# Operands formed a step ahead, another order of the seven products with eight PSUM banks, and output weights that stay split

## The chip, the cores and the metric

The kernel runs on one core of one Trainium2 chip. It has a matrix engine (TensorE, "PE" in the profile, its weight loads "PEld"), a vector engine (VectorE, "DVE"), a scalar engine (ScalarE, "ACT"), GpSimd ("POOL") and a sync engine ("SP") that here only starts DMAs. Each engine takes its instructions strictly in the order in which the kernel issued them. The metric is the device time of one execution in microseconds, the median over runs.

## The reference

One step of a decoder layer, for 1024 prompt tokens and 8 × 4 sample tokens that share the weights. The middle (convolution, state space and attention branches) is not touched by the change and is left out here.

```python
D_MODEL = 1024; D_FF = 2816
h = rmsnorm(x, g_pre_mix) * (1 + sc_m) + sh_m
merged = ...                                   # three branches of h @ w_in, each gated
x = x + g_m * rmsnorm(merged @ w_out, g_post_mix)
hf = rmsnorm(x, g_pre_ffn) * (1 + sc_f) + sh_f
gu = hf @ w_ffn_in                             # 1024 -> 2 * 2816
f = silu(gu[..., :D_FF]) * gu[..., D_FF:]
x = x + g_f * rmsnorm(f @ w_ffn_out, g_post_ffn)
```

## The kernel before

The 1056 tokens (1024 prompt, 32 sample) lie on the free axis in four chunks c of 264; features lie on the 128 partitions. Products are fp32 quality made of three matmuls of rounded operands: every weight tile and every activation tile is split into a high part (a ScalarE copy) and a low part (VectorE: the value less its high part), and PE adds high·high, high·low and low·high. So one 128 × 128 weight tile against one chunk is three matmuls of 128 × 264.

**The planner.** `run()` (L357-430) walks a list of atoms, each a group of matmuls into one PSUM bank. For each it issues the weight loads on SP, the split of weight units that come due (`split`, L382), the atom's matmuls, then the evacuation of the atom before (`pending`), and then lets side generators go on (`side.advance`): each yields a number of microseconds of atoms after which its next step is issued. The order of issue is the order on each engine. `dense` atoms have 24 matmuls, atoms of a job of the FFN's first matrix 12, atoms of its second matrix 33.

The change touches what is issued after 1122 us of the profile; there the stages are these.

- **Output projection** (L1957-1963): four chunks × eight tiles m of 128 output features, 24 matmuls each. Each of the 32 atoms loads, splits and uses its weight again (`split`: ScalarE `whi` L393, VectorE `wlo` L394), though the weights of c = 0 to 3 are the same. The evacuation `sq_gated` (L1805) squares the bank on ScalarE, writes the gated value `y` on ScalarE, and adds the square into `ss` on VectorE. When a chunk is through, `res_gen(c)` (L1825) makes the two RMS norms and the residual of that chunk: a small `s` matmul of `ss` with ones, a chain of 13 tiny VectorE instructions for the reciprocal root (L436-452), `rs_dg`, another `s` matmul, VectorE products and sums over `y` and `xc`, and the same again for the norm before the FFN. The four run one after another in a queue (`todo`, L1931). PSUM is shared as six banks z for atoms and two s for these small products.
- **FFN in, plain** (`plain_job`, L2003): four of the 22 column tiles as dense atoms, 16 atoms for token half p = 0 and then 16 for p = 1. `res_gen(2)` and `res_gen(3)` run beside the first 16.
- **FFN in, seven products** (`in_job`, L2030): 18 jobs. A job takes gate and up weights of one tile pair and forms 2 × 2 block products of halves with seven products q instead of eight (Strassen's way, in Winograd's form). Operand q is a half tile or a VectorE sum or difference of such (`make`, L2044; tile names `raw`, `ru`, `s`), which `halves` (L1982) splits into `wop`: ScalarE copies the high part, VectorE subtracts. Each operand serves two atoms (p = 0, 1) against the activations `ORDER[q]` (L1967). The evacuation (L2062) combines the products in `st`; at q = 6 follow Tanh, a product and a product (silu·up), and in every second job four subtractions and a store to DRAM `fd` from POOL.
- **FFN out, seven products** (L2146 on): products q = 0 to 5, each four tiles mi × two p atoms of 33 matmuls, then q = 6. Its weight operands come in three pieces per mi (`out_operand`, L2183), sums S kept in four tiles; its activations are read back from `fd` and split (`b_load` L2121, `b_split` L2133, lines L2135 and L310, names `mh`, `ml`, `xa`). `gated` (L2221) squares and gates a finished output, `last_gen(c)` (L2260) makes the last norm and residual, partly on POOL, and stores.

```python
RY = (4.5, 2.5, 4, 2)                                               # L46: the steps of res_gen
key = (p, {2: 0, 5: 3, 6: 4}.get(q, q))                             # L2092: products that share a bank
ORDER = ('B11', 'B21', 'T2', 'T3', 'T1', 'T4', 'B22')               # L1967
if q == 2: TT(g[:, h0], job['s'], g[:, h0], ALU.subtract)           # L2048, right before halves()
act.activation(out=w[:, 0:n], in_=src, func=AF.Copy, scale=scale)   # L1984, halves()
```

## Time and profile before

| | |
|---|---|
| median of 3 runs | 2056.93 us (2053.38 to 2059.02) |
| profiled execution | 2050.83 us, its span 2049.1 us |
| PE busy | 1910.2 us (93%), mean granted clock 0.966 |
| DVE busy | 1358.9 us (66%) |
| ACT busy | 730.8 us (36%) |
| POOL busy | 216.9 us (11%) |
| DMA | 288.50 MB, mean 141 GB/s |

PE is busy nearly throughout, and a busy PE is not one at full rate: its rows also last longer when it is fed late or when its clock is granted at the lower of its levels. The stretch that the change touches, 1122 us to the end, has to be read by stage.

### The profile page before, as it was taken

Reading aid. Unit: us, or ns where it says so; the run is one execution under the profiler, and the core shown is the slowest. Engines: PE = TensorE matmul, PEld = TensorE weight load, DVE = VectorE, ACT = ScalarE, POOL = GpSimd, SP = SyncE. Lnnn points to the kernel's source line nnn. Section 1 sums busy time; section 2 is a strip of 40 time slices with the busy share of each in tenths; the row PEclk is TensorE's granted clock in tenths of the full one; section 3 lists DMA queues with packets and bytes.
Section 4 is the critical chain, followed back from the end, with each engine's and each line's share of the span. In section 5 each row is a group of like instructions: output and inputs, shape, how many; then the busy total and the mean of one; then the engine's idle time right before and its main releaser. Section 6 shows DMA issues by size and latency. Waiting matters only on the chain. (4 is left out here: it accounts for less than half of the span.)

```text
span 2049.1 us, 33598 instructions
## 1 busy us (share of the span) xinstructions
PE 1910.2 (93%) x13440; PEld 1777.1 (87%) x13440; DVE 1358.9 (66%) x2795; ACT 730.8 (36%) x1418; POOL 216.9 (11%) x365
## 2 busy tenths in 40 slices
PE   8999999999998999998999888899999999999785
PEld 2899798798876899997999888899999999999785
DVE  5687684474474686565866677776666666666676
ACT  3422422422422542222233564433332333453442
POOL 0000001001010142213100000100000001101013
PEclk9999999999999999999999999999999999999897
DMA  7333133234354453327532555632232223666543
GB/s 288 81 104 107 45 135 136 80 107 144 119 199 179 174 165 122 109 90 219 150 106 82 176 196 194 214 124 99 79 115 95 79 84 123 233 200 235 164 159 120
DMA packets 90156, 288.50 MB, mean 141 GB/s; under 512 B 15876, under 2 KB 22116, under 8 KB 87312
## 3 DMA queue, kind: packets, MB, share of 16 engines
q1 hardware_dynamic: 53552, 144.79, 22.1%
q0 software_dynamic: 29104, 115.11, 16.2%
q10 hardware_dynamic: 7344, 26.47, 3.9%
q8 instruction: 105, 1.72, 0.3%
q14 instruction: 51, 0.42, 0.1%
HBM read 219.09 MB, written 68.15 MB: 140 GB/s over the span
## 5 line engine op out<-in xcount | busy, mean ns | idle before, releaser
L307 PE MATMUL z<-mh,wop 128*128 128x264 f32 x2024 | 401.1, 292 | 18.3 <-ACT mh L2135 9.6
L307 PE MATMUL z<-hh,whi 128*128 128x352 f32 x1152 | 379.7, 330 | 2.6 <-ACT hh L620 1.4
L307 PE MATMUL z<-hh,wlo 128*128 128x352 f32 x1152 | 372.5, 323 | 3.1 <-DVE wlo L394 3.1
L307 PE MATMUL z<-hl,whi 128*128 128x352 f32 x1152 | 372.2, 323 | 1.1 <-DVE hl L310 1.1
L307 PE MATMUL z<-ml,wop 128*128 128x264 f32 x1408 | 350.8, 291 | 3.2 <-DVE ml L310 3.2
L307 PEld LDWEIGHTS z<-mh,wop 128*128 128x128 f32 x2024 | 334.1, 196 | 20.9 <-ACT mh L2135 10.3
L394 DVE SCALAR_TENSOR_TENSOR wlo<-raw,whi 128x1024 fp32r<-128x1024 f32 x148 | 180.4, 1222 | 170.8 <-ACT whi L393 169.9
L307 PEld LDWEIGHTS z<-ml,wop 128*128 128x128 f32 x1408 | 250.9, 195 | 4.7 <-DVE ml L310 4.4
L307 PEld LDWEIGHTS z<-hh,whi 128*128 128x128 f32 x1152 | 218.7, 190 | 14.4 <-issue 6.9
L393 ACT ACTIVATE whi<-raw 128x1024 fp32r<-128x1024 f32 x148 | 156.1, 1056 | 189.1 <-PE z L307 158.6
L307 PEld LDWEIGHTS z<-hl,whi 128*128 128x128 f32 x1152 | 218.9, 190 | 3.1 <-DVE hl L310 2.0
L307 PEld LDWEIGHTS z<-hh,wlo 128*128 128x128 f32 x1152 | 218.1, 189 | 3.7 <-DVE wlo L394 3.7
L1503 DVE SCALAR_TENSOR_TENSOR ycv<-cub,vecs,ycv 128x1024 f32<-128x1024 f32 x120 | 153.9, 1282 | 3.1
L1984 ACT ACTIVATE wop<-raw 128x512 fp32r<-128x512 f32 x150 | 90.2, 614 | 177.8 <-DVE raw L310 98.9
L307 PE MATMUL z<-mh,whi 128*128 128x264 f32 x384 | 115.5, 301 | 4.6 <-ACT whi L393 4.6
L307 PE MATMUL z<-xa,wop 128*128 128x264 f32 x792 | 113.6, 293 | 4.0 <-ACT xa L2135 1.6
L307 PE MATMUL z<-mh,wlo 128*128 128x264 f32 x384 | 113.2, 295 | 2.2 <-DVE wlo L394 2.2
L307 PE MATMUL z<-ml,whi 128*128 128x264 f32 x384 | 112.5, 293 | 0.0
L307 PEld LDWEIGHTS z<-xa,wop 128*128 128x128 f32 x792 | 105.7, 196 | 5.3 <-ACT xa L2135 1.8
L310 DVE TENSOR_TENSOR wop<-raw,wop 128x512 fp32r<-128x512 f32 x90 | 61.9, 689 | 53.0 <-ACT wop L1984 52.8
L307 PEld LDWEIGHTS z<-mh,whi 128*128 128x128 f32 x384 | 76.3, 199 | 5.3 <-ACT whi L393 5.0
L307 PEld LDWEIGHTS z<-mh,wlo 128*128 128x128 f32 x384 | 75.9, 198 | 3.2 <-DVE wlo L394 3.1
(431 smaller groups left out, 3605.4 us busy)
## 6 DMA issues: line engine op xcount, KB each, us to landing
raw<-i_win SPq DMA_DIRECT2D x48, 512.0 KB, 3.7
raw<-i_wfi SPq DMA_DIRECT2D x43, 512.0 KB, 4.2
raw<-i_wfo SPq DMA_DIRECT2D x80, 256.0 KB, 3.1
fd<-ft POOLq DMA_DIRECT2D x22, 792.0 KB, 5.4
raw<-i_wmod SPq DMA_DIRECT2D x32, 512.0 KB, 4.3
raw<-i_wout SPq DMA_DIRECT2D x32, 512.0 KB, 3.8
gd<-g ACTq DMA_DIRECT2D x24, 528.0 KB, 2.9
g<-gd ACTq DMA_DIRECT2D x24, 528.0 KB, 4.8
```

Of the source, the lines that this page charges most:

```text
L307: return pe.matmul(out=out, lhsT=lhsT, rhs=rhs, start=start, stop=stop, **kw)
L310: dve.tensor_tensor(out=out, in0=a, in1=b, op=op)
L393: act.activation(out=hi[:, 0:n], in_=raw[:, 0:n], func=AF.Copy, scale=scale)
L394: dve.scalar_tensor_tensor(out=lo[:, 0:n], in0=raw[:, 0:n], scalar=scale, in1=hi[:, 0:n].bitcast(F32), op0=ALU.mult, op1=ALU.subtract)
L1503: dve.scalar_tensor_tensor(out=a_, in0=ub[:, k:k + TP], scalar=wv[:, k:k + 1], in1=a_, op0=ALU.mult, op1=ALU.add)
L1984: act.activation(out=w[:, 0:n], in_=src, func=AF.Copy, scale=scale)
```

## The change

Four edits. (1) `later` and `flush`: some instructions are no longer issued where they are written, but at the next operand's split or ahead of the next weight-using atom's matmuls: VectorE's low part of an operand or of an activation, the addition of squares, gating, Tanh and what follows it. A new function `pre` of an operand forms its sum or difference; it is issued when the operand *before* it is split. (2) `ORDER` is (B11, B21, T1, T2, T3, B22, T4), products that share a bank are now 0 and 3, 2 and 5, 4 and 6, Tanh follows q = 5, q = 2 is copied by ScalarE and q = 4 takes two VectorE additions; all eight PSUM banks are for atoms in this stage. (3) In the output projection the split weights of m = 4 to 7 stay in SBUF after c = 0 (`kept`); PSUM is shared four and four; the four `res_gen` run side by side, each started as its chunk ends, with other steps (`RY`); squares are added in pairs, and the last addition of `y` is left to PE, which takes two matmuls in place of one; `xc` lies in other tiles. (4) In the output stage S and the reloaded residual lie in twelve small tiles, `last_gen` is issued an atom later, and the loads and splits of the first activations are spread otherwise. In numbers, PE has 36 small matmuls more, DVE 48 instructions less, ACT 24 more, POOL 20 DMAs more and SP 12 weight loads less.

```diff
-RY = (4.5, 2.5, 4, 2)
+RY = (6, 3, 6, 2)
+    late_ops = []
+    def later(fn):
+        late_ops.append(fn)
+    def flush():
+        now = late_ops[:]
+        late_ops.clear()
+        for fn in now:
+            fn()
...
         def split(v):
             if op:
+                flush()
+                if v + 1 < len(units) and units[v + 1][3]:
+                    units[v + 1][3]['pre']()
                 parts[v] = wp.tile([128, 1024], F32R, tag=tags(v)[0], name="wop")
                 op['make'](parts[v])
                 return
             raw = raws.pop(v)
-            hi = wp.tile([128, 1024], F32R, tag="whi", name="whi")
-            lo = wp.tile([128, 1024], F32R, tag="wlo", name="wlo")
+            if keep:
+                hi, lo = keep()
+            else:
+                hi = wp.tile([128, 1024], F32R, tag="whi", name="whi")
+                lo = wp.tile([128, 1024], F32R, tag="wlo", name="wlo")
...
+            if a_.units:
+                flush()
             ps = a_.mm([parts[u] for u in a_.units])
...
-        open_psum(6, 2)
+        open_psum(4, 4)
...
         def rest():
-            if not first:
+            if i % 2 and i > 1:
                 TT(R_['ss', c], R_['ss', c], sq, ALU.add)
...
         TT(y[:, 0:4], y[:, 0:4], y[:, 4:8], ALU.add)
         TT(y[:, 0:2], y[:, 0:2], y[:, 2:4], ALU.add)
-        TT(y[:, 0], y[:, 0], y[:, 1], ALU.add)
         yield RY[2]
-        dg = rstd_bcast(rp, [y[:, 0, :]], 1024, EPS, 3)
+        dg = rstd_bcast(rp, halves_of(y), 1024, EPS, 3, place)
...
             if m == 7:
-                todo(res_gen(c), *([x_gen(0), x_gen(1)] if c == 3 else []))
+                R_['g', c] = side.add(res_gen(c))
+                if c == 3:
+                    R_['g', 4] = side.add(x_gens())
...
-            u = unit(flat(I['wout'][m]))
+            if c == 0 or m < 4:
+                u = unit(flat(I['wout'][m]), keep=kept(m) if m >= 4 else None)
+                if m >= 4:
+                    stay[m] = u
+            u = stay.get(m, u)
...
-    ORDER = ('B11', 'B21', 'T2', 'T3', 'T1', 'T4', 'B22')
+    ORDER = ('B11', 'B21', 'T1', 'T2', 'T3', 'B22', 'T4')
...
-            TT(w[:, 512:512 + n], src, w[:, 0:n].bitcast(F32), ALU.subtract)
+            later(lambda: TT(w[:, 512:512 + n], src, w[:, 0:n].bitcast(F32), ALU.subtract))
...
+        def pre(q):
+            def fn():
+                g, u = job['g'], job['u']
+                if q == 2:
+                    job['s'] = R_['fq'].tile([128, 512], F32, tag="s1", name="s1")
+                    TT(job['s'], u[:, h0], u[:, h1], ALU.add)
+                    TT(u[:, h0], g[:, h0], u[:, h0], ALU.subtract)
+                if q == 3:
+                    TT(g[:, h0], job['s'], g[:, h0], ALU.subtract)
+                if q == 5:
+                    TT(g[:, h1], g[:, h1], g[:, h0], ALU.subtract)
+            return fn
...
                 elif q == 5:
-                    TT(u[:, 0:LC], u2, z, ALU.add)
+                    TT(g[:, LC:2 * LC], u2, z, ALU.add)
+                    def act_on():
+                        act.activation(out=t, in_=g, func=AF.Tanh, scale=0.5)
+                        later(lambda: dve.scalar_tensor_tensor(out=t, in0=t, scalar=1.0, in1=g, op0=ALU.add,
+                                                               op1=ALU.mult))
+                    later(act_on)
                 else:
+                    TT(u[:, 0:LC], u2, z, ALU.add)
-                    TT(g[:, LC:2 * LC], u2, z, ALU.add)
-                    t = ft[:, 2 * b:2 * b + 2].rearrange("p a x -> p (a x)")
-                    act.activation(out=t, in_=g, func=AF.Tanh, scale=0.5)
-                    dve.scalar_tensor_tensor(out=t, in0=t, scalar=1.0, in1=g, op0=ALU.add, op1=ALU.mult)
-                    TT(t, t, u, ALU.mult)
-                    store(n, p)
+                    later(lambda: (TT(t, t, u, ALU.mult), store(n, p)))
...
-                    key = (p, {2: 0, 5: 3, 6: 4}.get(q, q))
+                    key = (p, {3: 0, 5: 2, 6: 4}.get(q, q))
...
         side.drain()
         late(1)
+        open_psum(8, 0)
...
-            if mi == 3 and q >= 5:
-                rest_now()
-                todo(last_gen(n2 if q == 5 else n1))
+                gated(n1, mi + 4, (lambda: todo(last_gen(n1))) if mi == 3 else None)
```

**The end of an FFN job on VectorE.** `ft` is silu·up being formed, its row of four the subtractions ahead of a store, `wop` the low part of an operand, `raw<-raw` the difference that is operand q = 6 (before) or q = 5 (after), `st<-st,z` the evacuations. Operands are split up to six ahead of PE, so the rows on `ft` belong to the job before. Before, from the low part of operand q = 4 to that difference:

```order
L310 TENSOR_TENSOR wop<-s_14273,wop 128x512
L310 TENSOR_TENSOR st<-st,z 128x264 x2
L2083 SCALAR_TENSOR_TENSOR ft<-ft,st 128x528
L310 TENSOR_TENSOR ft<-ft,st 128x528
L310 TENSOR_TENSOR ft<-ft 128x264 x4
L310 TENSOR_TENSOR wop<-raw,wop 128x512
L310 TENSOR_TENSOR st<-st,z 128x264
L2083 SCALAR_TENSOR_TENSOR ft<-ft,st 128x528
L310 TENSOR_TENSOR ft<-ft,st 128x528
L310 TENSOR_TENSOR ft<-ft 128x264 x4
L310 TENSOR_TENSOR raw<-raw 128x512
```

After, from that difference on:

```order
L310 TENSOR_TENSOR raw<-raw 128x512
L2147 SCALAR_TENSOR_TENSOR ft<-ft,st 128x528
L310 TENSOR_TENSOR wop<-raw,wop 128x512
L310 TENSOR_TENSOR st<-st,z 128x264 x2
L2147 SCALAR_TENSOR_TENSOR ft<-ft,st 128x528
L310 TENSOR_TENSOR ft<-ft,st 128x528
L310 TENSOR_TENSOR ft<-ft 128x264 x4
L310 TENSOR_TENSOR wop<-raw,wop 128x512
L310 TENSOR_TENSOR st<-st,z 128x264
L310 TENSOR_TENSOR ft<-ft,st 128x528
L310 TENSOR_TENSOR ft<-ft 128x264 x4
L310 TENSOR_TENSOR wop<-raw,wop 128x512
```

The difference now stands six rows ahead of the first subtractions and no longer right behind both rows of four.

**The operands of product five on VectorE.** `S<-raw,S` forms a piece of the operand, `wop<-S,wop` is its low part; the high part is ScalarE's in between. Before:

```order
L310 TENSOR_TENSOR ya<-ya,Gf 128x32
L310 TENSOR_TENSOR S<-raw,S 128x512
L1988 SCALAR_TENSOR_TENSOR wop<-S,wop 128x512
L310 TENSOR_TENSOR S<-raw,S 128x512
L1988 SCALAR_TENSOR_TENSOR wop<-S,wop 128x512
L310 TENSOR_TENSOR S<-raw,S 128x384
L1988 SCALAR_TENSOR_TENSOR wop<-S,wop 128x384
```

After:

```order
L310 TENSOR_TENSOR ss<-ss 128x528
L310 TENSOR_TENSOR S<-raw,S 128x512
L2046 SCALAR_TENSOR_TENSOR wop<-S,wop 128x512
L310 TENSOR_TENSOR S<-raw,S 128x384
L2046 SCALAR_TENSOR_TENSOR wop<-S,wop 128x512
L310 TENSOR_TENSOR S<-raw,S 128x512
L310 TENSOR_TENSOR ya<-ya,z 128x264
L310 TENSOR_TENSOR ya<-ya 128x264 x2
L2046 SCALAR_TENSOR_TENSOR wop<-S,wop 128x384
L310 TENSOR_TENSOR ml<-ml,mh 128x792
```

Before, each low part stands right behind the formation of its own piece; now the next piece's formation stands between the two.

**The second norm in the output projection on VectorE.** `y` is the squared residual, summed over its eight tiles; `ss` the sum of squares of the chunk that runs beside it. Before, in the fourth chunk:

```order
L310 TENSOR_TENSOR y<-y,s 128x1056
L310 TENSOR_TENSOR xc<-xc,y 128x1056
L394 SCALAR_TENSOR_TENSOR wlo<-raw,whi 128x1024
L310 TENSOR_TENSOR ss<-ss,sq_11882 128x264
L310 TENSOR_TENSOR y<-z,Gm 128x32
L310 TENSOR_TENSOR y<-y 128x1056
L310 TENSOR_TENSOR y<-y 128x528
L310 TENSOR_TENSOR y<-y 128x264
L310 TENSOR_TENSOR ss<-ss,sq_11891 128x264
L310 TENSOR_TENSOR y<-z,Gm 128x32
L394 SCALAR_TENSOR_TENSOR wlo<-raw,whi 128x1024
```

After, in the third chunk:

```order
L310 TENSOR_TENSOR y<-z,Gm 128x32
L310 TENSOR_TENSOR ml<-y,mh 128x1056 x2
L310 TENSOR_TENSOR y<-z,Gm 128x32
L310 TENSOR_TENSOR y<-y,s 128x1056
L310 TENSOR_TENSOR xc<-xc,y 128x1056
L310 TENSOR_TENSOR ss<-ss 128x528
L310 TENSOR_TENSOR y<-z,Gm 128x32
L310 TENSOR_TENSOR y<-y 128x1056
L310 TENSOR_TENSOR y<-y 128x528
L310 TENSOR_TENSOR y<-z,Gm 128x32
L310 TENSOR_TENSOR ss<-ss 128x528
L310 TENSOR_TENSOR y<-z,Gm 128x32
```

Before, a weight's low part `wlo` stands between these rows; now, in the second half of a chunk, none does, and the third addition of `y` is gone.

## Rows read from the trace of the kernel before

**Rows 1.** By stage: length, busy PE PEld DVE ACT POOL, PEclk, DMA share
```profile
1122.38:1306.75 184.37, 160.56 (x1218) 157.91 (x1217) 132.08 (x258) 96.43 (x161) 10.87 (x17) 0.93 0.57 187
1306.75:1353.21 46.46, 46.46 (x387) 46.46 (x386) 36.02 (x51) 15.96 (x22) 3.91 (x6) 1.00 0.66 231
1353.21:1747.91 394.70, 378.58 (x3026) 376.66 (x3025) 267.84 (x520) 127.46 (x242) 27.49 (x41) 0.97 0.29 97
1747.91:1885.87 137.96, 132.76 (x1059) 131.51 (x1057) 86.50 (x134) 64.76 (x113) 16.64 (x30) 0.98 0.63 211
1885.87:1925.10 39.23, 34.97 (x267) 34.25 (x265) 24.67 (x46) 14.00 (x24) 2.67 (x5) 0.91 0.62 207
1925.10:1978.47 53.37, 38.94 (x271) 36.90 (x271) 35.47 (x66) 25.29 (x44) 5.22 (x7) 0.86 0.56 179
1978.47:2031.30 52.83, 41.35 (x266) 39.35 (x267) 41.49 (x88) 17.31 (x36) 19.09 (x12) 0.82 0.41 134
2031.30:2049.10 17.80, 4.16 (x27) 3.15 (x26) 10.02 (x28) 3.10 (x7) 2.95 (x2) 0.70 0.24 91
```

**Rows 2.** Waits of PE from 1122.38 us to the end: total, times, longest
```profile
PE z L307 <- ACT st L2068: 16.1, 9, 1.8
PE s L307 <- DVE y L310: 15.1, 3, 6.0
PE s L307 <- DVE ss L310: 10.5, 3, 5.6
PE z L307 <- ACT mh L2135: 9.6, 3, 5.0
PE z L307 <- DVE wop L1988: 7.9, 7, 4.2
PE s L307 <- DVE rs_dg L463: 5.8, 3, 2.9
```

**Rows 3.** The page's group of the weights' low parts: busy, mean ns, idle
```profile
L394 DVE SCALAR_TENSOR_TENSOR wlo<-raw,whi 128x1024 fp32r<-128x1024 f32 x148 | 180.4, 1222 | 170.8 <-ACT whi L393 169.9
```

**Rows 4.** Timeline of VectorE, output projection: start, duration, [idle <- releaser]
```profile
1285.79 0.43 DVE L2022 SCALAR_TENSOR_TENSOR ft<-ft,z 128x264 f32<-128x264 f32 x1 [1.43 <-ACT ft L2021]
1286.13 2.46 DVE L310 TENSOR_TENSOR y<-y 128x1056 f32<-128x1056 f32 x3
```

**Rows 5.** Timeline of PE in the same place
```profile
1288.74 1.01 PE L307 MATMUL s<-cst,y 128*88 128x1 f32 x6 [5.86 <-DVE y L310]
```

**Rows 6.** Timeline of all engines at one end of an FFN job
```profile
1576.43 1.58 DVE L310 TENSOR_TENSOR ft<-ft 128x264 f32<-128x264 f32 x4
1577.93 0.68 DVE L310 TENSOR_TENSOR raw<-raw 128x512 f32<-128x512 f32 x1
...
1578.71 0.63 ACT L1984 ACTIVATE wop<-raw 128x512 fp32r<-128x512 f32 x1 [3.40 <-DVE raw L310]
1579.24 0.37 ACT L2068 ACTIVATE st<-z 128x264 f32<-128x264 f32 x1
...
1579.67 1.56 PE L307 MATMUL z<-xy,wop 128*128 128x264 f32 x10 [1.80 <-ACT st L2068]
```

**Rows 7.** Timeline of ScalarE at the start of the output stage
```profile
1765.89 0.39 ACT L2233 ACTIVATE ya<-z 128x264 f32<-128x264 f32 x1 [9.13 <-DMA fd<-ft]
```

**Rows 8.** Timeline of VectorE where product four begins
```profile
1890.48 0.69 DVE L310 TENSOR_TENSOR raw<-raw 128x512 f32<-128x512 f32 x1 [1.26 <-DMA raw<-i_wfo]
```

**Rows 9.** Timeline of VectorE in product five
```profile
1939.37 0.68 DVE L310 TENSOR_TENSOR S<-raw,S 128x512 f32<-128x512 f32 x1
1940.81 0.69 DVE L1988 SCALAR_TENSOR_TENSOR wop<-S,wop 128x512 fp32r<-128x512 f32 x1 [0.76 <-ACT wop L1984]
```

**Rows 10.** Timeline of VectorE and of POOL in product six
```profile
1985.97 0.70 DVE L2276 TENSOR_TENSOR ya<-ya,s 128x528 f32<-128x528 f32 x1 [0.58 <-ACT bs L2270]
...
1989.62 3.51 DVE L1988 SCALAR_TENSOR_TENSOR wop<-raw,wop 128x512 fp32r<-128x512 f32 x2
...
1989.09 1.76 POOL L2276 TENSOR_TENSOR ya<-ya,bs 128x528 f32<-128x528 f32 x1
```

More of the change, by code (lines that the diff above doesn't have):

```diff
@@ L369, in load @@
         def load(v):
-            src, n, scale, op = units[v]
+            src, n, scale, op, keep = units[v]
             if op:
@@ L428, in run @@
         if pending:
+            flush()
             pending()
+        while late_ops:
+            flush()
         side.drain()
@@ L453, in rsqrt_small, with rstd_bcast @@
         return y
-    def rstd_bcast(pool_, sq, nfeat, eps, nj=4):
+    def rstd_bcast(pool_, sq, nfeat, eps, nj=4, place=None):
         s = st()
@@ L461, in rstd_bcast @@
         r = rsqrt_small(pool_, s[0:88, 0:nj], 88, nj, 1.0 / nfeat, eps)
-        dg = pool_.tile([88, nj, 88], F32, tag="rs_dg", name="rs_dg")
+        dg = pool_.tile([88, nj, 88], F32, tag="rs_dg", name="rs_dg") if place is None else place()
         dve.tensor_tensor(out=dg, in0=ident[0:88, 0:88].unsqueeze(1).to_broadcast([88, nj, 88]),
@@ L1829, in res_gen, with place @@
         npr = LC if c < 3 else TP - 3 * LC
-        xc = rp.tile([128, 8, LC], F32, tag="xc", name="xc", bufs=1)
-        pool.dma_start(out=xc, in_=I['xQ'][c])
+        if c < 3:
+            t = (R_['fq'].tile([128, 8, LC], F32, tag="ft", name="xc") if c == 1 else
+                 rp.tile([128, 8, LC], F32, tag="xc", name="xc", bufs=1))
+            xc = [t[:, 0:4], t[:, 4:8]]
+        else:
+            xc = [parts4(R_['xb'].tile([128, T], F32, tag="xb", name="xc", bufs=4)) for _ in range(2)]
+        place = None
+        if c % 2:
+            def place():
+                t = R_['fq'].tile([128, 512], F32, tag="s1", name="rs_dg")
+                return t[0:88, 0:LC].rearrange("p (a b) -> p a b", a=3)
+        for h in range(2):
+            pool.dma_start(out=xc[h], in_=I['xQ'][c][:, 4 * h:4 * h + 4])
         yield RY[3]
-        dg = rstd_bcast(rp, [R_['ss', c]], 1024, EPS, 3)
+        dg = rstd_bcast(rp, halves_of(R_['ss', c]), 1024, EPS, 3, place)
         yield RY[0]
@@ L1929, in program, with todo @@
     queue = []
-    def todo(*gens):
-        queue.extend(gens)
+    def todo(gen):
+        queue.append(gen)
         if 'q' not in R_ or R_['q'] not in side.live:
@@ L1938, in todo, with x_gens @@
             R_['q'] = side.add(work())
+    def x_gens():
+        while ('B22', 1) not in X_:
+            yield 1.0
+        yield from x_gen(0)
+        yield from x_gen(1)
     def finish_res():
-        while ('B22', 1) not in X_:
-            side.step(R_['q'])
+        side.finish(R_['g', 3])
     def m_parts(k, c):
@@ L1951, in evac, with kept @@
                 R_['y', c] = R_['rp'].tile([128, 8, LC], F32, tag="y", name="y", bufs=3)
-            sq_gated(R_['rp'], c, m, m == 0, R_['y', c][:, m], ps[:, 0:LC], Gm, 2, 1, lsl(c))()
+            rest = sq_gated(R_['rp'], c, m, m, R_['y', c][:, m], ps[:, 0:LC], Gm, 2, 1, lsl(c))
+            rest() if m == 7 else later(rest)
             if m == 7:
-                todo(res_gen(c), *([x_gen(0), x_gen(1)] if c == 3 else []))
-        return evac
+                R_['g', c] = side.add(res_gen(c))
+                if c == 3:
+                    R_['g', 4] = side.add(x_gens())
+        return evac
+    def kept(m):
+        which = 'xa' if m < 6 else 'xb'
+        return lambda: [R_[which].tile([128, T], F32R, tag=which, name="keep", bufs=4)[:, 0:1024] for _ in range(2)]
+    stay = {}
     plain(lambda: None)
@@ L1966, in program, with operand @@
     F_ = {}
-    ORDER = ('B11', 'B21', 'T2', 'T3', 'T1', 'T4', 'B22')
+    ORDER = ('B11', 'B21', 'T1', 'T2', 'T3', 'B22', 'T4')
     opno = [0]
-    def operand(load, make, ahead):
+    def operand(load, pre, make, ahead):
         opno[0] += 1
-        return unit(None, op={'load': load, 'make': make, 'ahead': ahead, 'no': opno[0]})
+        return unit(None, op={'load': load, 'pre': pre, 'make': make, 'ahead': ahead, 'no': opno[0]})
     def gemm4(ps, w, x, ks, first, last, again=False):
@@ L2104, in open_st @@
         if p == 0:
-            F_['ft', p] = R_['fq'].tile([128, 8, LC], F32, name="ft")
+            side.finish(R_['g', 1])
+            F_['ft', p] = R_['fq'].tile([128, 8, LC], F32, tag="ft", name="ft")
         else:
@@ L2276, in last_gen @@
             tt(out=ya[:, ks], in0=ya[:, ks], in1=r, op=ALU.mult)
-            tt(out=xc[:, ks], in0=xc[:, ks], in1=ya[:, ks], op=ALU.add)
-            (act if last and i == 3 else sp).dma_start(out=O['yT'][c][:, ks], in_=xc[:, ks])
+            tt(out=xc[i], in0=xc[i], in1=ya[:, ks], op=ALU.add)
+            (act if last and i == 3 else sp).dma_start(out=O['yT'][c][:, ks], in_=xc[i])
             yield YF[2]
```

131 lines of the change are left out of this document (67 added, 64 removed), and 2 rows, old and new, of the table PLACE.

## The prediction

> **What bounds the kernel now.** I read the table by stage first, then the waits of PE, then the timelines around the longest of them. All work up to 1122 us is issued in the same order in both kernels, so only the stages in [rows 1] can move. The reader is to see three things there. The second plain half (1306.75 to 1353.21) shows the rate without waits: 384 matmuls in 46.46 us at a granted clock of 1.00, 0.121 us each. Every other stage is longer than its matmuls at that rate, and no stage has another engine near its length, except product six, where VectorE is busy for 41.49 of 52.83 us. So PE bounds, and each stage's loss is its length less the matmuls at that rate:
>
> - output projection and first plain half: 1152 matmuls make 139.4, it takes 184.37, lost 45.0;
> - FFN jobs: 3024 make 365.9, it takes 394.70, lost 28.8;
> - products 0 to 3 of the output: 1056 make 127.8, it takes 137.96, lost 10.2;
> - product 4: 264 make 31.9, it takes 39.23, lost 7.3; product 5: 53.37, lost 21.5; product 6: 52.83, lost 20.9;
> - the tail, 17.80, has nearly no matmuls (27 PE instructions).
>
> The waits [rows 2] say what the loss is: nine waits for an `st` copy of ScalarE, 1.8 us each (FFN jobs); three each for `y`, `ss` and `rs_dg` of VectorE (the norms); `mh` and `wop` (the output stage). The rest of the loss, some 60 us, is matmuls at a lower granted clock: it is 0.93, 0.97, 0.91, 0.86 and 0.82 in the stages that wait and 1.00 in the one that does not [rows 1]. The level falls in stages in which PE has stood still, so a wait removed gives back its own length and some of the slow matmuls behind it (in the FFN jobs 28.8 lost for 16.1 waited).
>
> **The change part by part.**
>
> *Output projection, 45.0 lost.* Twelve of its weight splits go, with VectorE's `wlo` and ScalarE's `whi` and the loads. VectorE's busy time here is 132.08 us [rows 1]; the twelve are 1.22 us each [rows 3], 14.7 in all, and 28 additions of squares of about 0.43 (a 264-wide step in [rows 4]) become 12 of 528 at about 0.70 [rows 10], 3.6 less. It then has some 114 of 139.4 us, and waits in its queue are shorter. The long waits are for `y`: PE stood 5.86 us [rows 5] while VectorE first waited for ScalarE (1.43) and then added the squares in 2.46 [rows 4]. The addition of the last pair is now PE's own, and the side generators start their reductions where PE has a further step to run. What is late next: at the end of each chunk the chains of two norms stand behind one another on VectorE. One chain costs PE 5.8 / 3 = 1.9 us where it shows [rows 2]; four places at 1.9, and about 1 us of slow matmuls behind each, leave 12. Four z banks in place of six leave four atoms of 2.9 us for an evacuation, three of them free, against 0.85 us of ScalarE work; I price that at nothing, covered by those 8.7 us. If ScalarE is held for longer by a norm's squares and its eight gatings, it costs up to what is left of them. Gain 33; bounds 20 (only the `y` waits of 15.1 and a third of that in clock) and 40.
>
> *FFN jobs, 28.8 lost.* [Rows 6] show the knot: four subtractions ahead of a store hold VectorE for 1.58 us, twice per second job; then the difference for an operand (0.68), then ScalarE, 3.40 idle for it, copies that operand, and only then the `st` copy that empties the bank which PE adds its third product to: 1.80 us of PE. The new order uses that bank for q = 3 and not for q = 2, two atoms later: 2 × 12 × 0.121 = 2.9 us more room against the 1.8 needed. The difference also stands ahead of the subtractions, and Tanh a product earlier. So all nine waits go, and the 12.7 us of slow matmuls with them, apart from the first job's start-up: 4 stay. Added are 36 ScalarE copies, about 0.37 each [rows 6], 13.3 us on an engine that is busy for 127.46 of 394.70, beside PE; if that cover went, they would be added whole. Eight z banks cost nothing, since no norm runs here. Gain 24; bounds 17 (the nine waits) and 27.
>
> *Output stage, products 0 to 3, 10.2 lost.* ScalarE's first copy into `ya` waits 9.13 us for a store whose subtractions were late [rows 7]; with the job's end earlier on VectorE it is released sooner. Sums for q = 2 and 3 are formed a piece ahead. Gain 6, bounds 2 and 9.
>
> *Products 4 and 5, 28.8 lost.* A piece goes VectorE sum (0.68), ScalarE copy, VectorE low part (0.69): from 1939.37 to 1941.50 in [rows 9], 2.1 us, of which VectorE is idle for 0.76. With the next piece's sum in that gap, three pieces take 3 × 1.37 = 4.1 on VectorE rather than 6.2, and the activation's `mh` and low part behind them come 2 us sooner; `mh` made PE wait 9.6 in three [rows 2]. `last_gen` is issued an atom later, so the `ss` reduction that stopped PE for up to 5.6 [rows 2] has 4.0 us more. Product 5 gains 16 of 21.5. In product 4 a new wait appears: each sum takes two loads, and it now stands in VectorE's queue ahead of the low part of the piece before; where the load is late (1.26 in [rows 8]), that low part, the evacuations behind it, and PE's next atom are late too. I take three of product 4's 7.3 as gained. Bounds: 5 and 24 together.
>
> *Product 6, 20.9 lost.* Its operands are plain weights, so nothing is formed ahead. VectorE is busy 41.49 us [rows 1], partly because steps stretch beside POOL: two low parts take 3.51 us next to a POOL product of 1.76, where one alone takes 0.69 [rows 9, 10]; a step with one operand in PSUM keeps its 0.70 [rows 10]. The four pairs of square additions save VectorE about 0.6 us and nothing else goes, so the stage can come down to about VectorE's 41 us and some waiting: 43. Gain 10, bounds 0 and 18.
>
> The Trainium skill, page "SBUF — State Buffer", section "SBUF: two separate sides", says that a VectorE step with two SBUF inputs and a GpSimd step that reads SBUF exclude each other for a whole instruction. The trace agrees: 3.51 us for two, near twice the POOL step of 1.76. By that rule the stretch cannot go while POOL keeps its eight steps, and the 41 us is a floor; without it the stage could come to 34.
>
> *Tail.* The same chain as before, with three tiny matmuls more: 0, bounds −1 and +1.
>
> Sum: 33 + 24 + 6 + 16 + 3 + 10 = 92 us off the profiled 2050.83 (span 2049.1 and 1.7 around it), 1958.8. The median shown is 6.1 above that execution, so 1965 as a median. The bounds add to 44 and 118; they are not all low or all high together. All else that the diff moves (other tiles for `xc`, small S tiles, POOL's 20 more DMAs, the loads of 512 KB that go) I cost at nothing: the DMA share is 0.29 to 0.66 [rows 1] beside PE; if that cover failed, it would show as the rival on loads.
>
> **The rivals.**
>
> 1. *Sums formed ahead wait for loads.* Products 2 to 5 have 4 × 4 × 3 = 48 pieces; if half of them wait 1.26 us as in [rows 8], 30 us go: 1995. For it: VectorE's queue is in order and the loads share DMA with activations (share 0.62 in product 4). Against: only products 2 and 4 need two loads per piece.
> 2. *Product 6 and half of 5 keep their loss*, since VectorE's norms and POOL still meet there: 1965 + 10 + 8 = 1983. For: 41.49 of 52.83 busy. Against: half of the wait of product 5 is `mh`, not VectorE's load.
> 3. *The norms side by side crowd ScalarE and VectorE*, and with four banks PE waits for evacuations: only 20 of 45 gained, 1978.
> 4. *Product 6 comes near the rate*, as POOL's steps no longer meet the low parts: 1965 − 9 = 1956.
> 5. *Slower.* Low parts of the FFN jobs are now issued one split later. If the six operand tiles ahead run dry, each of the 18 × 7 = 126 operands delivers its low part one VectorE step (0.69) late: 87 us, and the 24 are not gained either: 1965 + 24 + 87 = 2076. It decides from 0.59 us per operand on (then 2063, 0.3% over the median). Against: no wait of PE in these jobs is for `wop` now, the longest are for `st`, and VectorE is busy for 68%.
> 6. *No change*, if removed waits only move to another operand of the same atoms: about 2055. Against: the plain half shows PE at full rate beside 36.02 of 46.46 us of VectorE.
>
> **How the numbers follow.** Forecast 0.54, with its own range 1950 to 1980; rival 1 0.13; 2 0.10; 3 0.06; 4 0.10; 5 0.04; 6 0.03. The range 1944 to 1996 takes in the forecast, rivals 2 to 4 and most of rival 1. Differences under 0.3% can't be told from none here (three runs lie within 5.6 us). Faster 0.93, same 0.03, slower 0.04.
>
> **What would show it.** Right: no wait of PE for an `st` copy in the jobs, their stage at 368 to 373 us and clock 1.00; output projection and first plain half at 148 to 155; product 5 near 37; `wop` sums without ScalarE idle in between; low parts in product 6 still stretched beside POOL. Wrong: PE waiting for `wop` in products 2 to 5 with VectorE idle for `raw` (rival 1), for evacuations in the output projection (rival 3), or product 6 still above 50 (rival 2).

## The result

The changed kernel takes 1982.52 us (median of 4 runs, 1981.16 to 1983.15), the kernel before 2057.97 beside it (4 runs): ratio 0.9635, 95% interval 0.9616 to 0.9653. That is 75 us less; the forecast was 92 less, 1965, with a range from 1944 to 1996 (the narrower one of the forecast alone, 1950 to 1980, is just missed). The profiled execution took 1981.16 us (span 1979.4), 69.7 less than the profiled one of before.

The table by stage of the changed kernel, in the cuts of [rows 1] (length, then busy time and instructions of PE, PEld, DVE, ACT and POOL, granted clock, DMA share, GB/s):

```profile
1125.32:1288.19 162.87, 155.63 (x1267) 153.72 (x1265) 115.72 (x226) 84.38 (x148) 15.66 (x25) 0.98 0.55 188
1288.19:1341.66 53.47, 50.79 (x385) 50.01 (x386) 37.96 (x54) 18.04 (x26) 3.90 (x6) 0.94 0.44 156
1341.66:1708.14 366.48, 366.48 (x3026) 366.48 (x3025) 269.95 (x517) 142.48 (x277) 27.61 (x41) 1.00 0.31 104
1708.14:1838.16 130.02, 128.99 (x1059) 128.15 (x1058) 86.42 (x132) 65.26 (x114) 16.71 (x30) 1.00 0.69 229
1838.16:1877.60 39.44, 34.77 (x266) 34.56 (x265) 25.69 (x48) 15.89 (x29) 3.21 (x6) 0.91 0.57 189
1877.60:1911.47 33.87, 32.18 (x266) 31.97 (x265) 28.76 (x53) 21.80 (x39) 9.61 (x14) 1.00 0.72 247
1911.47:1959.72 48.25, 42.58 (x307) 40.46 (x306) 37.75 (x86) 19.12 (x37) 18.73 (x15) 0.89 0.49 161
1959.72:1979.40 19.68, 2.68 (x17) 1.69 (x16) 11.13 (x25) 2.16 (x5) 6.30 (x4) 0.63 0.29 110
```

| stage | before [rows 1] | after | gain | forecast |
|---|---|---|---|---|
| output projection, first plain half | 184.37 | 162.87 | 21.5 | 33 |
| second plain half | 46.46 | 53.47 | −7.0 | 0 |
| FFN jobs | 394.70 | 366.48 | 28.2 | 24 |
| products 0 to 3 | 137.96 | 130.02 | 7.9 | 6 |
| product 4 | 39.23 | 39.44 | −0.2 | 3 |
| product 5 | 53.37 | 33.87 | 19.5 | 16 |
| product 6 | 54.9 | 48.3 | 6.6 | 10 |
| tail | 15.7 | 19.6 | −3.9 | 0 |
| all ahead of 1122 us | 1122.38 | 1125.32 | −2.9 | 0 |

In the rows for product 6 and the tail, product 6 ends in both kernels where its last matmul starts. The last boundary of [rows 1], at 2031.30, lies 2 us ahead of that, inside the last atom, and counts that atom's end to the tail. PE's timeline, before and after:

```profile
2033.33 0.28 PE L307 MATMUL z<-mh,wop 128*128 128x264 f32 x1
...
1959.79 0.28 PE L307 MATMUL z<-mh,wop 128*128 128x264 f32 x1
```

The last row of the table is no effect of the change: that part is issued alike, and in the runs below it ends anywhere from 1119.5 to 1128.4 us. Products 4 and 5 share loads and have to be read together: 92.6 before, 73.3 after. In the nine runs below that leave them alone their sum is 72.4 to 74.9, while product 4 takes 35.6 to 39.5 and product 5 33.6 to 39.1.

The waits of PE in the changed kernel, answering to [rows 2] (total us, times, longest):

```profile
PE s L307 <- DVE ss L310: 7.2, 3, 3.8
PE z L307 <- DVE ml L310: 7.0, 3, 4.7
PE s L307 <- DVE rs_dg L489: 4.0, 2, 3.0
PE z L307 <- DVE ft L2080: 3.9, 3, 1.9
PE z L307 <- ACT wop L2042: 2.8, 1, 2.8
...
PE s L307 <- DVE y L310: 1.5, 2, 0.9
```

The nine waits for `st` are gone, those for `y` fell from 15.1 to 1.5, those for `mh` from 9.6 to 0.3. New are those for `ft` (an evacuation of a plain job); those for `ml` grew (before 3.2 us in five, the longest 1.3), and one for a `wop` of ScalarE is longer than before (2.2 us in two). In the FFN jobs the granted clock is 1.00 where it was 0.97, so the slow matmuls behind the waits went with them.

### The profile page after: what moved, and what is told of

Its sections match the earlier page's. It is cut to its first block, busy times and chain, and to the rows that moved or that the text cites. A ratio compares the mean times of both kernels' runs of the same rounds, so it can differ in the third digit from the quotient of the medians.

```text
span 1979.4 us, 33713 instructions
## 1 busy us (share of the span) xinstructions
PE 1890.1 (95%) x13512; PEld 1761.9 (89%) x13512; DVE 1339.0 (68%) x2747; ACT 735.7 (37%) x1442; POOL 230.2 (12%) x385
## 5 line engine op out<-in xcount | busy, mean ns | idle before, releaser
L307 PE MATMUL z<-ml,wop 128*128 128x264 f32 x1400 | 342.1, 286 | 7.1 <-DVE ml L310 7.0
L307 PEld LDWEIGHTS z<-mh,wop 128*128 128x128 f32 x2032 | 327.5, 191 | 6.3 <-ACT wop L2042 3.3
L415 DVE SCALAR_TENSOR_TENSOR wlo<-raw,whi 128x1024 fp32r<-128x1024 f32 x132 | 160.9, 1222 | 146.3 <-ACT whi L414 145.2
L307 PEld LDWEIGHTS z<-ml,wop 128*128 128x128 f32 x1400 | 243.0, 190 | 8.0 <-DVE ml L310 7.9
L414 ACT ACTIVATE whi<-raw 128x1024 fp32r<-128x1024 f32 x132 | 139.2, 1056 | 180.8 <-PE z L307 166.1
L310 DVE TENSOR_TENSOR wop<-raw,wop 128x512 fp32r<-128x512 f32 x90 | 61.9, 688 | 44.5 <-ACT wop L2042 44.5
L307 PE MATMUL z<-mh,whi 128*128 128x264 f32 x288 | 85.8, 298 | 0.8 <-DVE ft L310 0.6
L307 PE MATMUL z<-ml,whi 128*128 128x264 f32 x288 | 83.1, 289 | 0.0
L307 PE MATMUL z<-mh,wlo 128*128 128x264 f32 x288 | 82.8, 288 | 0.0
L307 PE MATMUL z<-zh,whi 128*128 128x264 f32 x256 | 73.6, 287 | 0.0
L307 PE MATMUL z<-zl,whi 128*128 128x264 f32 x256 | 72.8, 284 | 0.0
```

What stands on the lines that cost most here:

```text
L307: return pe.matmul(out=out, lhsT=lhsT, rhs=rhs, start=start, stop=stop, **kw)
L310: dve.tensor_tensor(out=out, in0=a, in1=b, op=op)
L414: act.activation(out=hi[:, 0:n], in_=raw[:, 0:n], func=AF.Copy, scale=scale)
L415: dve.scalar_tensor_tensor(out=lo[:, 0:n], in0=raw[:, 0:n], scalar=scale, in1=hi[:, 0:n].bitcast(F32), op0=ALU.mult, op1=ALU.subtract)
```

## The experiments

Stage lengths below are from each run's profile, cut as above.

**What made the second plain half longer: x_wait, bank6.** The generator that forms the sums of the FFN's input reads `y` back from DRAM; the step `YX` lies between those loads and their first use. VectorE's first steps on it, in the timeline of the changed kernel (start, duration, [idle before <- releaser]):

```profile
1286.54 1.26 DVE L310 TENSOR_TENSOR y<-y 128x1056 f32<-128x1056 f32 x1 [7.33 <-DMA y<-xh]
...
1314.00 1.26 DVE L310 TENSOR_TENSOR y<-y 128x1056 f32<-128x1056 f32 x1 [7.46 <-issue]
```

VectorE stands 7.3 and 7.5 us at the head of its queue (the second is put down to its issue, but the loads of that operand land at 1313.92, as it starts), and the evacuations behind it are late. PE's timeline at the first of the two:

```profile
1288.19 0.51 PE L307 MATMUL z<-xa,whi 128*128 128x264 f32 x2 [1.83 <-DVE ft L2080]
```

That wait ends as the second half begins. Inside the half PE waits for two more `ft` and one further step, some 2.7 us; the rest of the loss is slow matmuls (granted clock 0.94).

```diff
 x_wait
-        yield YX
+        yield YX + 7.0
 bank6
-        open_psum(4, 4)
+        open_psum(6, 2)
```

> The changed kernel, with one number other: the generator that forms the operand sums of the FFN input lets 7 us more pass between its two loads of y and its first use of them (11.2 for 4.2). In the profile of the changed kernel those loads land 10.7 and 11.5 us after their issue, VectorE stands 7.3 and 7.5 us at its first use, and the second plain half takes 53.5 us against 46.5 before. Theory (VectorE held at that load keeps the evacuations back, and four banks don't last that long): both stands of VectorE shrink below 1 us, the second plain half falls to 47 to 48 us and the total by 6 to 8 us, to about 1975. Rival (the half is longer for the loads' own traffic, or for the fewer banks at any time): the half stays at 52 to 54 us and the total within 2 us of 1982.5.

Measured: 1974.40 us (1970.15 to 1977.09), ratio 0.9589 (0.9566 to 0.9612). The second plain half takes 46.56 us, as before the change; all 7 us are back. One stand of 2.8 us stays, the other is gone, and PE waits for neither.

> The changed kernel with PSUM shared six and two in the output projection and the plain jobs, as before, and not four and four. Theory (four banks are what turns VectorE's stand at the load of y into waits of PE): the second plain half falls to 46.5 to 48 us although VectorE still stands 7 us at its loads; the output projection itself grows by 0 to 6 us, since four norms side by side now share two banks. Rival (the banks do not matter, VectorE's late work itself is what PE waits for): the half stays at 52 to 54 us.

Measured: 1980.85 us, ratio 0.9627 (0.9607 to 0.9648). The half takes 51.89 us. VectorE still stands 7.3 and 7.4 us; PE with six banks runs on past the evacuation and stops at the next thing in VectorE's queue, a weight's low part, as its timeline shows:

```profile
1300.45 0.39 PE L307 MATMUL z<-xa,wlo 128*128 128x264 f32 x1 [2.40 <-DVE wlo L415]
...
1326.40 0.39 PE L307 MATMUL z<-xa,wlo 128*128 128x264 f32 x1 [1.67 <-DVE wlo L415]
```

So the stand of VectorE is the cause: x_wait gives back 6.9 us and two banks more only 1.6. The banks mostly decide which instruction behind the stand PE waits for. My theory for this run, that four banks turn the stand into a wait, fell. The output projection and the first plain half did not grow with two banks for the norms.

**What the kept weights are worth: no_keep.**

```diff
-            if c == 0 or m < 4:
-                u = unit(flat(I['wout'][m]), keep=kept(m) if m >= 4 else None)
-                if m >= 4:
-                    stay[m] = u
-            u = stay.get(m, u)
+            u = unit(flat(I['wout'][m]))
```

> The changed kernel with the kept weights undone: each of the 32 atoms of the output projection loads and splits its weight, 12 loads, 12 ScalarE and 12 VectorE splits (1.22 us each) more. Theory (what stood in the way there were VectorE's queue and its splits): 132 us of VectorE in 184 us before, so the 14.7 us come back as waits at the norms: output projection and first plain half 162.9 to 168 to 175 us, total 1988 to 1995. Rival (the norms side by side, the reductions on PE and the deferral made the gain, and the splits lie beside PE's work): 162 to 166 us, total within 3 us of 1982.5.

Measured: 2002.34 us, ratio 0.9733 (0.9714 to 0.9751), 20 us above the changed kernel. Output projection and first plain half take 180.6 us (23.15 for chunk 0 and 157.44), 17.7 more. The waits of PE in chunks 1 to 3 (total us, times, longest):

```profile
PE s L307 <- DVE ss L310: 6.6, 3, 3.5
PE z L307 <- DVE y L310: 5.0, 3, 3.3
PE z L307 <- DVE wlo L415: 2.3, 3, 0.8
PE z L307 <- ACT whi L414: 1.8, 2, 1.5
```

The splits stood in the way, and by more than their own 14.7 us of VectorE: they wait for ScalarE too (17.2 us of VectorE's idle time, longest 2.1), and the reductions of `ss` come behind them. Their twelve loads did not: ScalarE waits 0.4 us for one there.

**The two norms at a chunk's end: first_later, wait_later.**

```diff
 first_later
-        yield RY[3]
+        yield RY[3] + 6.0
 wait_later (with x_wait's edit)
+        yield RY[3] + (6.0 if c < 3 else 0.0)
```

> The changed kernel with 6 us more ahead of the first norm of each chunk in the output projection (8 for 2), some two atoms. Theory (at the end of a chunk two chains of 14 small VectorE instructions, the second norm of one chunk and the first of the next, stand back to back, and PE waits 1.6 to 1.7 us at the second one's reduction behind them): those waits on ss go, the first atoms of chunks two and three lose 1 to 2 us and not 3, total 3 to 6 us less. Rival (the norm only ends later, and something behind it is late in turn, such as the loads of y or the last chunk's norms in the plain half): total the same or up to 5 us more.

Measured: 1986.58 us, ratio 0.9655 (0.9638 to 0.9673). Chunks 1 to 3 take 79.9 us and not 85.9; the two plain halves take 115.1 and not 107.3.

> The changed kernel with two earlier edits together: 7 us more between the loads of y and their first use (alone it brought 8 us: 1974.4), and 6 us more ahead of the first norm of chunks 0 to 2 (alone, in all four chunks, it took 5.9 us off chunks 1 to 3 and gave 7.9 back in the plain jobs, whose loads of y came later: 1986.6). Theory (the two losses are separate, what came back in the plain jobs was the last chunk's delay and the same stand of VectorE at the loads): output projection from chunk 1 on 79 to 81 us, first plain half 52 to 54, second 46.5, total 1968 to 1972. Rival (PE pays for the norms wherever they are put): the plain halves grow by what the chunks gain, total 1973 to 1976.

Measured: 1976.04 us, ratio 0.9593 (0.9562 to 0.9625). Chunks 1 to 3 again 79.9, second plain half 46.56, but the first one 60.65 where 53.78 stood. PE waits for `y` there:

```profile
PE s L307 <- DVE y L310: 5.2, 3, 3.1
PE z L307 <- DVE y L310: 2.3, 1, 2.3
```

The rival holds: what the chunks gain the first plain half pays.

**What undid the knot in the FFN jobs: old_order2, own_step, order_own.**

```diff
 old_order2
-    ORDER = ('B11', 'B21', 'T1', 'T2', 'T3', 'B22', 'T4')
+    ORDER = ('B11', 'B21', 'T2', 'T3', 'T1', 'T4', 'B22')
-                    key = (p, {3: 0, 5: 2, 6: 4}.get(q, q))
+                    key = (p, {2: 0, 5: 3, 6: 4}.get(q, q))
 ...
 own_step
-                if v + 1 < len(units) and units[v + 1][3]:
-                    units[v + 1][3]['pre']()
+                op['pre']()
-            later(lambda: TT(w[:, 512:512 + n], src, w[:, 0:n].bitcast(F32), ALU.subtract))
+            TT(w[:, 512:512 + n], src, w[:, 0:n].bitcast(F32), ALU.subtract)
 ...
```

The lines not shown move the sums, the evacuations and Tanh to the places that the old order gives them, and issue the other form of the low part at once. order_own has both edits.

> The changed kernel with the old order of the seven operands in the FFN jobs: B11 B21 T2 T3 T1 T4 B22, banks shared by products 0 and 2, 3 and 5, 4 and 6, Tanh after product 6; the tiles in which the activations lie, the deferral of low parts and stores, the sums a step ahead and the eight banks stay as changed. The FFN jobs take 394.7 us before and 366.5 after. Theory 1 (the knot at a job's end is the bank that product 2 needs again so soon): nine waits for an st copy of 1 to 2 us come back, the stage takes 380 us or more. Theory 2 (the knot was VectorE's row, the difference behind the subtractions for the store, and the deferral and the step ahead undo it by themselves): the stage stays at 366 to 370 us, the total within 3 us of 1982.5.

Measured: 1982.90 us; the jobs take 366.97 us and PE waits for nothing in them. Theory 2 holds: the order of the operands is not needed in the jobs. Behind them it is worth something: products 0 to 3 take 132.5 for 130.0 (128.7 to 130.8 in the runs that leave the jobs and them alone), product 0 alone 36.45 for 32.62 and 37.37 before.

> The changed kernel with the operands in one go as before: an operand's sum is formed at its own split and its low part issued right behind ScalarE's copy, no step apart; order, banks, kept weights and the rest as changed. Theory (VectorE's idle time between sum, copy and low part cost the output stage its products 2 to 5): product 5 goes from 33.9 us back to 40 to 50, products 0 to 3 from 130 to 134 to 138, the FFN jobs stay within 3 us of 366.5; total 1995 to 2005. Rival (product 5 was freed by the later start of the last norm and of its reductions): product 5 stays at 34 to 36 us, total within 4 us of 1982.5.

Measured: 1990.21 us (2 runs), ratio 0.9680 (0.9647 to 0.9714). The jobs take 366.48, products 0 to 3 131.9, product 5 43.5, products 4 and 5 together 79.0 for 73.3, and product 6 51.5 for 48.3 (47.8 to 48.8 in the runs that leave it alone). The theory holds for product 5 and the jobs; products 0 to 3 and the total lie below what it gave. VectorE is back to forming, waiting and splitting, as in [rows 9]:

```profile
1881.13 0.68 DVE L310 TENSOR_TENSOR S<-raw,S 128x512 f32<-128x512 f32 x1
1882.57 0.69 DVE L2045 SCALAR_TENSOR_TENSOR wop<-S,wop 128x512 fp32r<-128x512 f32 x1 [0.76 <-ACT wop L2041]
```

And PE, in the waits of that stretch, is back to one of 5.0 us for `mh`, as long as the longest of its kind in [rows 2]:

```profile
PE z L307 <- ACT mh L2203: 5.0, 1, 5.0
```

In the changed kernel the same steps have no gap:

```profile
1882.03 0.55 DVE L310 TENSOR_TENSOR S<-raw,S 128x384 f32<-128x384 f32 x1
1882.50 0.68 DVE L2046 SCALAR_TENSOR_TENSOR wop<-S,wop 128x512 fp32r<-128x512 f32 x1
```

> The changed kernel with two edits undone together: the old order of the operands in the FFN jobs and the operands in one go (sum at its own split, low part right behind ScalarE's copy). Each alone left the jobs at 366.5 to 367.0 us. What stays of the change in the jobs is eight banks and Tanh, its products and the store deferred by a split or an atom. Theory 1 (the deferral of Tanh, products and stores, or the two banks more, undoes the knot): the jobs stay at 366 to 370 us. Theory 2 (order and step ahead each suffice, and one of the two is needed): waits for an st copy come back at the second jobs and the stage takes 380 to 395 us.

Measured: 2026.59 us (2 runs), ratio 0.9854 (0.9834 to 0.9875). The jobs take 398.4 us, and the nine waits are back:

```profile
PE z L307 <- ACT st L2130: 21.2, 9, 2.6
```

So the order and the step ahead each suffice, and one is needed; the eight banks and the deferral of Tanh, products and stores alone bring nothing here (398.4 against 394.7 before).

**Products 4 and 5: gate.** VectorE in the changed kernel, as product 4 begins, answers to [rows 8]:

```profile
1840.74 0.56 DVE L310 TENSOR_TENSOR raw<-raw 128x384 f32<-128x384 f32 x1 [2.70 <-DMA raw<-i_wfo]
...
1847.58 0.69 DVE L310 TENSOR_TENSOR raw<-raw 128x512 f32<-128x512 f32 x1 [5.68 <-DMA raw<-i_wfo]
```

```diff
+            if o == 10:
+                if i == 3:
+                    plain(gate)
+                    b_loads((o, 0), (o, 1), (o, 2), (o + 1, 0), (o + 1, 1))
...
```

`gate` is a small POOL step that reads product 4's first output.

> The changed kernel with five loads of activations that product 5 will need held back: in the trace of the changed kernel POOL starts them as product 4 begins, as soon as their buffers are free, beside product 4's own weights, two loads for each piece, which then land 7.5 to 9.0 us after issue where 2.6 is usual; a small POOL step on the first finished output of product 4 now stands ahead of them, and their splits come two atoms later. Theory (VectorE waits 2.7 and 5.7 us at the head of its queue for those weights, and PE 4.7 us for it): the weights land in under 5 us, these waits fall to under 1 us, products 4 and 5 together from 73.3 to 66 to 69 us, total 4 to 7 us less than 1982.5. Rival (the weights are late by themselves, or the held loads come late for product 5): products 4 and 5 together stay at 72 us or more.

Measured: 1987.64 us (1982.72 to 1991.06), ratio 0.9652 (0.9623 to 0.9682). Product 4 takes 33.0 us, near the rate; product 5 takes 42.1; together 75.1, no less than in the runs that leave both alone. The waits of VectorE for product 4's weights are as many and as long as in the changed kernel (there 10.8 us in three):

```profile
DVE raw L310 <- DMA raw<-i_wfo: 11.3, 3, 7.1
```

The loads do slow the weights: by issue and landing in the traces product 4's weights land 5.1 to 9.0 us after issue beside them in the changed kernel, and 2.4 to 4.2 while they are held. But held back, they run into product 4's later weights, which then land 6.2 to 7.8 us after issue (longest wait 7.1 us for 5.7), and PE pays in product 5. Whether it pays there for that or for the later splits was not separated; the theory that another time for these loads saves 4 to 7 us fell.

**Product 6 and the tail: pool_store, no_pool.**

```diff
 pool_store
-            (act if last and i == 3 else sp).dma_start(out=O['yT'][c][:, ks], in_=xc[i])
+            (act if last and i == 3 else sp if last else pool).dma_start(out=O['yT'][c][:, ks], in_=xc[i])
 no_pool
-            on_pool = i in (PL if not last else (3,))
+            on_pool = i in (() if not last else (3,))
```

> The changed kernel with the stores of the result y (but for the last chunk) issued from POOL's queue and not SP's. In the profile of the changed kernel weight loads of product 6 stand on SP behind such stores, which wait for POOL's sums; ScalarE then waits up to 3.8 us for a weight and PE 2.8 us for ScalarE. Theory (SP's order is what holds the weights): loads issue some 3 us earlier, that wait of PE goes, product 6 falls from 48.3 to 44 to 46 us, total 2 to 4 us less. Rival (the weights are late because four loads of the residual from POOL run in the same 6 us, or VectorE's stretched low parts set the pace in any case): product 6 within 1 us of 48.3.

Measured: 1980.02 us, ratio 0.9631 (0.9608 to 0.9655). Product 6 falls from 48.3 to 44.5 us, as the theory has it, and PE's 2.8 us for a `wop` of ScalarE are gone. In the waits of the changed kernel's SP, from 1905 us on, its stores stand for POOL:

```profile
SPq L2352 <- POOL x L2351: 20.8, 6, 7.8
```

Three weights behind such stores are issued from 1942.59 to 1943.55 and land 5.1 to 6.7 us later; in this run they are issued from 1938.95 to 1942.69 and land 3.0 to 3.6 us later. That they land faster has another reason, which the edit brings with it: the stores now hold back POOL's own loads of the residual, by 2.1 to 3.3 us. So what SP's order is worth by itself was not separated from that traffic.

The tail grows from 19.6 to 22.0 us (19.6 to 21.3 in the runs that leave it alone). VectorE's last two sums of squares in the timeline of this run:

```profile
1958.85 3.91 DVE L310 TENSOR_TENSOR ss<-ss 128x528 f32<-128x528 f32 x2
```

The same two in the changed kernel:

```profile
1960.88 2.84 DVE L310 TENSOR_TENSOR ss<-ss 128x528 f32<-128x528 f32 x2
```

One alone, earlier in the changed kernel:

```profile
1880.21 0.70 DVE L310 TENSOR_TENSOR ss<-ss 128x528 f32<-128x528 f32 x1
```

At the end they stand beside POOL's products, on the path to the last norm.

> The changed kernel with the last norms of three chunks wholly on VectorE and none of their steps on POOL (the last chunk's piece on POOL stays). Theory (POOL's steps stretch VectorE's low parts beside them from 1.75 to 4.0 us for three): the stretched groups shrink to 1.75, VectorE loses 2.2 us less at each of two norms and takes over four steps of about 0.7 to 0.8 for each, 2.9 us; product 6 within 2 us of 48.3, since the price only changes hands. Rival (the stretch has another cause than POOL, such as DMA traffic): the groups of three stay near 4.0 us and product 6 grows by 5 us or more.

Measured: 1986.04 us (2 runs), ratio 0.9660 (0.9631 to 0.9690). Product 6 takes 47.2; of the 3.5 us that the whole takes more, 2.2 lie in the first stage, which this edit leaves alone. Three low parts behind a last norm, in VectorE's timeline of the changed kernel:

```profile
1938.68 3.99 DVE L2046 SCALAR_TENSOR_TENSOR wop<-raw,wop 128x512 fp32r<-128x512 f32 x3
```

And in this run, without POOL:

```profile
1947.36 1.76 DVE L2046 SCALAR_TENSOR_TENSOR wop<-raw,wop 128x512 fp32r<-128x512 f32 x3
```

The stretch is POOL's doing and the price changes hands, as expected. The Trainium skill ("SBUF — State Buffer", section "SBUF: two separate sides") has such VectorE steps and POOL's shut each other out; 3.99 with POOL at work against 1.76 without agrees.

**best** has x_wait's and pool_store's edits, and leaves the last pair of squares to PE:

```diff
-            if i % 2 and i > 1:
+            if i % 2 and i > 1 and not (G is Gf and c == 2 and i == 7):
-        dg = rstd_bcast(yp, halves_of(R_['ss', c]), 1024, EPS, 3)
+        dg = rstd_bcast(yp, halves_of(R_['ss', c]) + (halves_of(R_['sq', c]) if c == 2 else []), 1024, EPS, 3)
```

> The changed kernel with three edits more: 7 us more between the loads of y and their first use (alone 1974.4); the stores of y of three chunks from POOL's queue and not SP's (alone product 6 from 48.3 to 43.7 us, and the tail from 19.7 to 22.8, since VectorE's last two sums of squares stood beside POOL's steps, 3.91 us for two); and the last pair of squares of the last chunk summed by PE (six small matmuls more, some 1.1 us) and not by VectorE. Theory: second plain half 46.5, product 6 44 us, the tail 20.5 to 22 us; total 1968 to 1972. Rival (the tail gives back what product 6 gains, as in the run of that edit alone): 1972 to 1976.

Measured: 1972.45 us (5 runs, 1967.65 to 1973.03), ratio 0.9583 (0.9567 to 0.9600): faster than both kernels, 0.5% below the changed one. Second plain half 46.6, product 6 44.8, tail 22.0. The rival holds: the tail gives back more than half of product 6's gain, and most of what this kernel gains is x_wait's (1974.40 alone).

## Why the prediction was right, and by how much it was off

The sign and the mechanism held: PE bounds, its waits went, the clock rose with them. Four terms of the sum fell short, by 11.5, 7.0, 3.2 and 7.3 us; three came out 9.6 better, and 2.9 lie ahead of the stages: 22.3 between 92 and 69.7. (As medians 17.5 are missing, since the profiled execution of before lay 6.1 us under the median shown and that of after 1.4.) That misses of both signs partly cancel is luck, and so is that rival 2's 1983 comes nearest: its mechanism did not come, for products 4 and 5 gained the whole 19.

*Output projection, 33 forecast, 21.5 measured.* The waits for `y` went as forecast, and not through the kept weights: in no_keep, too, PE's reductions wait 2.5 us for `y` and not 15.1. The kept weights carry 17.7 of the 21.5. Mis-sized was what stays: the sum left 12 us, it is 23.5. Four chunk ends were priced at 2.9 each; the stretches behind them (chunks 1 to 3, first plain half) lose 2.4, 6.6, 7.3 and 7.3 us against the rate. (The 1.9 taken for a chain is the mean of the three waits for `rs_dg` in [rows 2], of which one lies in this stage and two in the output stage.) PE's waits are 7.2 us of the 23.5. A larger part was left out of the sum: PE's own small matmuls, which the 45.0 lost held too and which could not go. Among PE's groups of instructions in this stage, changed kernel:

```profile
L307 PE MATMUL s<-rs_dg,cst 88*128 88x264 f32 x16 | 4.9, 385 | 0.0
L307 PE MATMUL s<-cst,ss 128*88 128x1 f32 x48 | 4.4, 219 | 4.0 <-DVE ss L310 3.4 <-DVE y L310 0.6
L307 PE MATMUL s<-cst,y 128*88 128x1 f32 x48 | 4.2, 214 | 0.9 <-DVE y L310 0.9
```

That is 13.5 us of busy time, 10.9 before. The additional ones, for which I charged nothing, lie on PE's path: a reduction takes 1.07 us where one that is fed in time took 0.56, and the eight of this stage 8.6 for 6.0. PE's timeline, changed kernel:

```profile
1203.00 1.07 PE L307 MATMUL s<-cst,y 128*88 128x1 f32 x12
```

And the kernel before:

```profile
1188.02 0.56 PE L307 MATMUL s<-cst,ss 128*88 128x1 f32 x6
```

The gain is near rival 3's size (20 of 45). Its norms that crowd VectorE are part of what stayed: the reductions of `ss` wait 3.4 us in this stage, and first_later takes 6 us off the chunks. Its waits for evacuations are little of it: with six banks for the atoms (bank6) the stage takes 159.3 us, and 161.7 to 165.0 in the runs that leave it alone.

*Second plain half, 0 forecast, 7.0 lost.* This is the step that failed: "I price that at nothing, covered by those 8.7 us". I looked only at ScalarE as what could hold an evacuation. It was VectorE, at the loads of `y`: 7.3 and 7.5 us and a step of 1.26 behind each, as long as that cover; x_wait gives all of it back. Before, VectorE stood there too (5.1 and 3.4 us) and PE did not notice. By the traces the first stand grew because VectorE came to it 3.5 us after the issue of the later load and not 6.8 (the load took 10.7 us, before 12.0), the second because its load took 11.5 us and not 6.4. Why that load was slower was not separated.

*FFN jobs, 24 forecast, 28.2 measured.* Right, but my reason was half of it: I gave it first to the 2.9 us more room at the bank. old_order2 takes this room away and loses 0.5 us; the step ahead alone does the same. The 4 us that I left for the first job's start-up did not stay: 366.48 is 0.6 over the rate's 365.9.

*Products 0 to 3, 6 forecast, 7.9 measured.* The store that ScalarE's first copy waits for lands 14.7 us after the start of product 0, before 17.9, sooner as the prediction has it. Here the new order counts: in old_order2 it lands after 17.0 us, and product 0 loses 3.8 of the 4.8 us that it gained.

*Products 4 and 5, 19 forecast, 19.3 measured.* That the sum meets the forecast is partly luck: the forecast gave product 4 three of it, and product 4 gained nothing in the profiled run; how the two share the time varies by 4 us and more in runs that leave them alone. Rival 1's wait came. VectorE's waits for weights in the output stage of the changed kernel:

```profile
DVE raw L310 <- DMA raw<-i_wfo: 12.8, 4, 5.7
...
DVE S L310 <- DMA raw<-i_wfo: 10.0, 8, 4.2
```

That is 22.8 us in twelve places (before 2.7 in two), near the 30 of rival 1 but on VectorE: PE waits 6.4 us in products 4 and 5, for `ml`. The step apart is worth 5.6 of the 19.3 (own_step; 4.1 against the slowest of the other runs); the rest, among the later last norm, the deferred gating and the other places of the splits, was not taken apart.

*Product 6 and tail, 10 forecast, 2.7 measured.* The floor that I took, VectorE's 41 us, was not what bound, and no floor: VectorE is busy 37.75 of 48.25, with POOL at work as long as before (18.73 us for 19.09; [rows 1] has twelve POOL steps there, not the prediction's eight). The weights came late behind stores on SP and beside loads of the residual (pool_store). The deferred low parts, which the prediction gave no part here, are worth some 3 us (own_step). The tail, priced at nothing, lost 3.9: the last two sums of squares, in pairs now, met POOL (2.84 us for some 1.4), and the twelve small matmuls behind them take 1.11 for 0.60. The rest of it was not taken apart.

Rival 5, the slower side, had nothing for it: PE waits for nothing in the jobs. Two slips of the sum: with the tail its bounds add to 43 and 119, and the "some 60 us" put down to the clock hold those small matmuls too.

## What to carry to other kernels

When an engine's queue is in order, price every instruction that waits for a load by all that stands behind it on that engine, evacuations of other atoms too, and ask for how long the slowest load can take there, not its usual time. An edit that takes work from one engine and gives a little to the bound one is not free: count those instructions at the bound engine's price. Where two edits each cure the same stall, undoing one shows nothing; undo both before calling either the cause.

## What the runs showed of the hardware

Two VectorE sums of SBUF operands took 2.84 and 3.91 us beside POOL's products, where one alone takes 0.70. The product with one operand in PSUM kept its 0.70 in the kernel before, at 1985.97 [rows 10], while POOL ran this:

```profile
1986.03 1.34 POOL L2276 TENSOR_TENSOR ya<-ya,bs 128x528 f32<-128x528 f32 x1 [19.33 <-ACT bs L2270]
```

A load of 1 MB from POOL's queue landed 10.7 to 11.5 us after issue with another load, a store and weights in flight, and 5.3 us in the kernel before, at 1325.99, where the next one was issued 4.2 us later.
